# Eight depth pairs by seven products in the late heads, and the weights' parts in two buffers and a third one by phase

## The chip, the cores and the metric

The kernel runs on one core of a Trainium2 chip. The metric is the device time of one execution in microseconds (us), the median of several runs. A profile is one such execution. Its engines are PE (TensorE, the matrix products; PEld is its loading of weights), DVE (VectorE), ACT (ScalarE), POOL (GpSimd, hardly used) and SP (SyncE, which issues the DMAs).

## The reference

A trunk of two layers on 512 tokens of width 2048, all in float32. The first layer is an mLSTM with 8 heads, the second a band attention that reads one K and V, computed from the first layer's result (kv_w). Only the first matters here:

```python
def mlstm_mixer(h, w_in, conv_w, conv_b, gate_b, g_head, w_out):
    proj = h @ w_in
    qk = jax.nn.silu(causal_conv(proj[..., :A_V0], conv_w, conv_b))
    v = proj[..., A_V0:A_O0]
    o = proj[..., A_O0:A_Z0]
    z = proj[..., A_Z0:A_G0]
    ...
    ht = mlstm_chunkwise(heads(qk[..., :A_QK], A_DK), heads(qk[..., A_QK:], A_DK), heads(v, A_DV), li, lf)
    ht = rmsnorm(ht, g_head.reshape(A_HEADS, A_DV)).reshape(Bn, S, A_INNER)
    y = jax.nn.sigmoid(o) * ht * jax.nn.silu(z)
    return y @ w_out
```

Each head has q and k of 256 columns, and v, o and z of 512.

## The kernel before

**Weights.** All weights lie in one stream of pieces of up to 128 x 1024 in the order of their use (stream, L60). wpiece (L188) takes the next one: a DMA into wr, a cast on ACT to the high part wh (L182), and a subtraction on DVE for the low part wl (L183). A product of two float32 matrices is three matmuls, high by high, high by low and low by high (mm3). wh and wl each have three buffers in the pool wp (L146), wr has two, and in some phases every third piece takes its wr from a pool of that phase (spare).

**Products by seven.** proj_s (L273) computes two column tiles at once. For a depth pair (two depth steps of 128) it either takes eight products as they are ("eight", 12 matmuls of 512 columns) or seven with sums of the weights and of the inputs, after Strassen and Winograd ("seven", 21 matmuls of 256). The weights' sums are made in wpiece: L207, L208 and L209 on DVE, then a cast and a subtraction for their parts wsh and wsl. The results come together in four accumulators D, C, A and B, and go to SBUF at L322 to L331. HEAD_PAIRS says how many of the eight depth pairs of a head's call go by seven: 7, the other one by eight, in the call's first piece. The other three pieces have two pairs by seven each ("merged").

**Heads.** The loop over h runs through 8 heads. Heads up to 3 (HALF) have q, k in other ways; head 3 makes the input's sums h1s on the way (head_sums, L598) and brings its o and z calls up by RAMP from 4 to 7 pairs. Heads 4 to 7 each make six calls of proj_s: q, k (names zq) and four for o and z (names zo), with V between (proj_b, four accumulators; its weights have one difference a piece, L214). After q and k stands the convolution (L547 to L549, then SiLU at L552).

**End of a head.** den gives dd, the four numerators ps_n go through L752 (square) and L753 (scaling of zo), the squares' sum sqs is split to sp_q, two matmuls make ps_q, and then comes a chain on one tile dd, in the pool t1: L759, L760 (DVE), a square root (ACT, L761), a reciprocal (DVE, L762), four products zo by dd (L764), each followed by a DMA that writes it to ysc.

**After head 7.** The pool t1 is closed with phA, and a_w_out follows: pieces 290 and up, y read back from ysc (yr), split into y, and ps_y. Piece 290 meets y0_0, the next one y0_1, and so on; the first needs nothing of head 7.

**Order.** Each engine runs its own queue in order. Within the program a scheduler sets that order, by priorities (high_priority, AHEAD = 300). A pool's memory may be that of an earlier pool: a tile then waits for the last use of the tiles that lay there (reuse_waits="tile").

Of the kernel before, what the change touches and what calls it, by code (L numbers as in the profile page):

```python
# [9 lines left out]
F32 = mybir.dt.float32  # L10
F32R = mybir.dt.float32r
# [4 lines left out]
P = 128  # L16
# [24 lines left out]


KEY_PAIRS = [6, 7, 8, 8, 8, 8, 8, 8]
HEAD_PAIRS = 7
RAMP = [4, 5, 6, 7]
HALF = 3
ATT_PAIRS = 8
# [85 lines left out]
def hybrid_trunk(ctx, tc, xT, xN, c, adaT, cols, wst, wg, ext, kc, out):  # L133
    nc = tc.nc
    order = stream()

    const = ctx.enter_context(tc.tile_pool(name="const", bufs=1))
# [5 lines left out]
    def pool(name, bufs=1, **kw):  # L143
        return tc.tile_pool(name=name, bufs=bufs, reuse_waits="tile", **kw)

    wp = ctx.enter_context(tc.tile_pool(name="wp", bufs=3, side="right"))  # L146

    ysc = dram.tile([NH, P, 4, S], F32, name="ysc")
    gsc = dram.tile([2, NH, S], F32, name="gsc")
# [8 lines left out]

    cl = const.tile([P, NCOL], F32, name="cl")
    kcs = const.tile([P, 144], F32, name="kcs")  # L160
    ones_f = const.tile([P, P], F32, name="ones_f")
    cst = const.tile([P, 4], F32, name="cst")
    mod = const.tile([P, 128], F32, name="mod")
    amul = const.tile([P, 3 * KT], F32, name="amul")
# [1 line left out]
    ssq = const.tile([P, 16], F32, name="ssq")  # L166
    rsn = const.tile([P, 4], F32, name="rsn")
    ssum = const.tile([P, S], F32, name="ssum")
    nc.vector.memset(ones_f, 1.0)
    nc.vector.memset(cst[:, 0:1], EPS)  # L170
    nc.vector.memset(cst[:, 1:2], 1.0)
    eps_c, one_c = cst[:, 0:1], cst[:, 1:2]
# [10 lines left out]
        nc.vector.tensor_tensor(lo, src, hi.bitcast(F32), op=ALU.subtract)  # L183

    ahead = [0]
    spare = [None]

    def wpiece(mat, groups=(), pl=None, bufs=(2, 2), diff=False):  # L188

        i, at = wpos
        m, blocks = order[i]
        assert m == mat
        n = sum(w for _, _, w in blocks)
        wpos[:] = i + 1, at + P * n
        with tc.high_priority(ahead[0]):
            own = spare[0] and i % (RAW_BUFS + 1) == 0
            raw = (spare[0] if own else wp).tile([P, 1024], F32, tag="raw", name=f"wr{i}", bufs=1 if own else RAW_BUFS)[:, :n]
            nc.sync.dma_start(raw, wst[at : at + P * n].rearrange("(p n) -> p n", p=P))  # L200
            ts = []
            c0 = 0
            for j, ns in enumerate(groups):
                w = ns * P
                r = raw[:, c0 : c0 + 4 * w]
                t = pl.tile([P, 3 * w], F32, tag="ws", name=f"ws{i}_{j}", bufs=bufs[0])
                nc.vector.tensor_tensor(t[:, : 2 * w], r[:, w : 3 * w], r[:, : 2 * w], op=ALU.subtract)  # L207
                nc.vector.tensor_tensor(r[:, w : 2 * w], t[:, w : 2 * w], r[:, :w], op=ALU.add)  # L208
                nc.vector.tensor_tensor(t[:, 2 * w :], r[:, 3 * w :], r[:, w : 2 * w], op=ALU.subtract)  # L209
                ts.append(t)  # L210
                c0 += 4 * w
            if diff:
                t = pl.tile([P, n // 2], F32, tag="ws", name=f"ws{i}", bufs=1)
                nc.vector.tensor_tensor(t, raw[:, n // 2 :], raw[:, : n // 2], op=ALU.subtract)  # L214
                ts.append(t)
            hi = wp.tile([P, 1024], F32R, tag="hi", name=f"wh{i}")[:, :n]
            lo = wp.tile([P, 1024], F32R, tag="lo", name=f"wl{i}")[:, :n]
            split(hi, lo, raw)
            out = [(hi, lo)]
            for j, t in enumerate(ts):  # L220
                sh = pl.tile(list(t.shape), F32R, tag="wsh", name=f"wsh{i}_{j}", bufs=bufs[1])
                sl = pl.tile(list(t.shape), F32R, tag="wsl", name=f"wsl{i}_{j}", bufs=bufs[1])
                split(sh, sl, t)
                out.append((sh, sl))
        return out
# [47 lines left out]
    def proj_s(mat, xs, ss, f, z1, z2, name, pl, bufs, at={}, merged=False, other=False):  # L273

        D, C, A, B = [(newa if other and n != "d" else newp)(f"ps_{n}{name}") for n in "dcab"]
        pieces = pair_pieces(f, merged)
        begun = set()
        h0, h1_ = slice(0, 256), slice(256, 512)  # L280
        for i, (sk, nk) in enumerate(pieces):
            if i in at:
                at[i]()
            main, *extra = wpiece(mat, [len(ks) for ks in sk], pl, bufs)

            def acc(ps, cols, parts, b, x, last):
                start = id(ps) not in begun
                begun.add(id(ps))
                w = slice(b * P, (b + 1) * P)
                mm3(ps[:, cols], parts[0][:, w], parts[1][:, w], x[:, 0, :], x[:, 1, :], start, last)  # L290

            def eight():
                b0 = 4 * sum(len(ks) for ks in sk)
                for m, k in enumerate(nk):
                    for j in range(2):
                        for t, ps in enumerate((A, B)):
                            acc(ps, slice(0, S), main, b0 + 4 * m + 2 * j + t, xs[2 * k + j], False)

            def seven(g, ks):
                ns = len(ks)  # L300
                b0 = 4 * sum(len(u) for u in sk[:g])
                end = i == len(pieces) - 1 and g == len(sk) - 1
                for ps, cols, t, at_, x, last in (
                    (D, h1_, 0, 1, lambda k: ss[k][1], False),
                    (D, h0, 0, 0, lambda k: xs[2 * k][:, :, h0], end),
                    (C, h0, 1, 1, lambda k: ss[k][2], False),
                    (C, h1_, 1, 0, lambda k: ss[k][0], end),
                    (A, h0, 0, 3, lambda k: xs[2 * k + 1][:, :, h0], False),
                    (A, h1_, 1, 2, lambda k: xs[2 * k + 1][:, :, h1_], end),
                    (B, h0, 0, 2, lambda k: ss[k][3], end),  # L310
                ):
                    if i == 0 and g == 0 and ps is B:
                        eight()
                    for j, k in enumerate(ks):
                        acc(ps, cols, extra[g] if t else main, (0 if t else b0) + at_ * ns + j, x(k), last and j == ns - 1)

            if i:
                eight()
            for g, ks in enumerate(sk):
                seven(g, ks)  # L320
        with tc.high_priority(AHEAD):
            nc.scalar.copy(z1[:, 0, :], D[:, h0])  # L322
            nc.vector.tensor_tensor(z2[:, 1, :], z1[:, 0, :], D[:, h1_], op=ALU.add)
            nc.vector.tensor_tensor(z1[:, 1, :], z2[:, 1, :], C[:, h0], op=ALU.add)
            nc.vector.tensor_tensor(z2[:, 0, :], z2[:, 1, :], C[:, h1_], op=ALU.add)
            nc.vector.tensor_tensor(z2[:, 1, :], z1[:, 1, :], C[:, h1_], op=ALU.add)
            nc.vector.tensor_tensor(z1, z1, A.rearrange("p (a t) -> p a t", a=2), op=ALU.add)
            if f < KT // 2:
                nc.vector.tensor_tensor(z2, z2, B.rearrange("p (a t) -> p a t", a=2), op=ALU.add)
            else:  # L330
                nc.vector.tensor_tensor(z2[:, 0, :], z2[:, 0, :], B[:, h0], op=ALU.add)  # L331
# [42 lines left out]
    phA = ExitStack()  # L374
    tp = phA.enter_context(pool("t1", bufs=3, side="right"))
    mst = ExitStack()
    q1p = mst.enter_context(pool("q1", side="right"))
    ap_ = mst.enter_context(pool("ada", side="right"))

    scB = ap_.tile([P, D], F32, name="scB")  # L380
# [1 line left out]
    acp = hst.enter_context(pool("acc"))  # L382
    st = ExitStack()
    sp = spare[0] = st.enter_context(pool("start"))
    ADA_BUFS = 3

    def ada_load(i, j, p, n, pin=lambda ins: ins):
# [30 lines left out]
    for q in range(4):  # L418
        t = sp.tile([P, 4, S], F32, name=f"xt{q}")
# [45 lines left out]
    h1 = []  # L465
# [130 lines left out]
    h1s = []  # L596
# [10 lines left out]

    def pair(c, name, other, f=HEAD_PAIRS, at={}):
        z1, z2 = (acp.tile([P, 2, 256], F32, tag="so", name=f"{name}_{i}", bufs=6) for i in range(2))
        proj_s("a_w_in", h1, h1s, f, z1, z2, name, hq, (1, 2), at, True, other)  # L610
        return [z.rearrange("p a t -> p (a t)") for z in (z1, z2)]

    def scores(h, j, qk, pr, nm, nmd, tot):
# [30 lines left out]
    for h in range(NH):  # L644
# [20 lines left out]
        if h == HALF:  # L665
            while loaded or pending:
                background(3)
            spare[0] = None
            mst.close()
            hqst = ExitStack()  # L670
            hq = hqst.enter_context(pool("hq", side="right"))
# [13 lines left out]
        at = {8 + 2 * j: lambda j=j: scores(h, j, qk, pr, nm, nmd, tot) for j in range(4)} if h else {}  # L685
# [11 lines left out]
        for m in range(4):  # L697
            with tc.high_priority(AHEAD):
                if m < 3:
                    t = hp.tile([P, 2, S], F32R, tag="qk", name=f"v{h}_{m}", bufs=4)  # L700
                    split(t[:, 0, :], t[:, 1, :], pv[m])
                else:
                    t = hp.tile([P, S], F32, tag="nm", name=f"v{h}_{m}")
# [6 lines left out]
        for i in range(4):  # L710
            if h >= HALF:
                f = HEAD_PAIRS if h > HALF else RAMP[i]
# [58 lines left out]
    hqst.close()  # L771
    hst.close()
    phA.close()


    kst = ExitStack()
# [142 lines left out]
    for pair, ms in enumerate(PAIRS):  # L919
        for g in range(1, 4):  # L920
            at = scale_steps(4, 12, 20, *([28] if g < 3 else [])) if pair == 0 else {}
            if pair == 0 and g == 3:
                at[28] = lambda: (scale_sums(), amul_cols(2, 48 + KT, GPRE + KT))
            if pair == 1 and g == 1:
                at = {2: lambda: residual(0), 4: lambda: residual(1)}
                at |= {20 + 4 * i: lambda i=i: turned(0, [i], False) for i in range(3)}
            if pair == 1 and g == 2:
                at = {2: lambda: turned(0, [3], False)}
# [62 lines left out]
    for i in range(KT // 2):  # L991
        z = zp.tile([P, 4, 256], F32, tag="z", name=f"zk{i}")
        ready = len(hs)
        at = {2: input_sums} if ready < KT // 2 else {}
# [8 lines left out]
    for g in range(2, 4):  # L1003
        n = -(-ATT_PAIRS // 2)
# [280 lines left out]
```

## Time and profile before

| | us |
|---|---|
| median of 3 runs | 2791.75 (2791.1 to 2793.53) |
| profiled execution | 2792.15 |
| its span | 2789.7 |
| PE busy | 2760.0 |
| DVE busy | 2200.9 |
| ACT busy | 1392.4 |

The span is the time from the first to the last instruction in the trace; 2.45 us of the execution lie around it. A row of a timeline has the start, the duration, engine, line and operation, out<-in, how many instructions are put together, and in brackets the idle time before it with what ended it. A matmul's duration overlaps the next one's, so PE's pace is read from start to start. Rows of groups have the busy time in all, the mean of one in ns, and the idle time ahead of them. Times are from the span's start.

### The profile page before, as it was taken

How to read it: one execution, taken by the hardware profiler on the slowest of the kernel's cores; microseconds unless marked ns; L12 is line 12 of the kernel's file. 1: busy time of each engine (PE TensorE's matmuls, PEld its weight loads, DVE VectorE, ACT ScalarE, POOL GpSimd, SP SyncE). 2: the span in 40 equal slices, each digit the busy share in tenths (PEclk: the TensorE clock that was granted, in tenths of full speed). 3: DMA queues.
4: the chain of work that ended last, by engine and by line, in shares of the span. 5: the costliest groups of instructions: out<-in, count | busy, mean ns of one | idle time of the engine just before them, and what ended most of it. 6: DMA issues, size and time to landing. Idle time of an engine off the chain costs nothing.

```text
span 2789.7 us, 42543 instructions
## 1 busy us (share of the span) xinstructions
PE 2760.0 (99%) x16184; PEld 2448.2 (88%) x16184; DVE 2200.9 (79%) x3647; ACT 1392.4 (50%) x2016; POOL 0.2 (0%) x4
## 2 busy tenths in 40 slices
PE   7999999999999999999999999999999999999998
PEld 5887888888998989989999888888999899999887
DVE  6986978769897887878967667567986698989676
ACT  4235524234555554555646344568534466666523
POOL 0000000000000000000000000000000000000000
PEclk9999999999999999999999999999999999999999
DMA  8975697865232332332325788878534533334687
GB/s 290 309 261 181 213 314 254 301 231 174 99 107 100 104 115 91 106 106 99 113 91 196 231 294 298 259 254 292 185 137 174 174 128 125 123 130 128 219 308 243
DMA packets 185015, 527.10 MB, mean 189 GB/s; under 512 B 19893, under 2 KB 38357, under 8 KB 184169
## 3 DMA queue, kind: packets, MB, share of 16 engines
q1 hardware_dynamic: 184810, 524.38, 55.6%
q8 instruction: 126, 2.06, 0.3%
q14 instruction: 79, 0.65, 0.1%
HBM read 490.69 MB, written 38.85 MB: 190 GB/s over the span
## 4 chain that ended last, share of the span: by engine, by line
PE 91%; DVE 4%; DMA 2%; ACT 1%; issue 1%; SPq 0%; DVEq 0%; ACTq 0%
PE ps_y L228 19%; PE ps_v L228 12%; PE ps_azo L228 5%; PE ps_o L228 4%; PE ps_kv L228 4%; PE ps_czo L228 3%; PE ps_dzo L228 3%; PE ps_az L228 3%; PE ps_cz L228 3%; PE ps_dz L228 3%; PE ps_qk L228 3%; PE ps_z L228 3%; PE ps_l L228 3%; PE ps_bzo L228 3%; PE ps_s L228 2%; PE ps_lead L228 2%
## 5 line engine op out<-in xcount | busy, mean ns | idle before, releaser
L182 ACT CAST wh<-wr 128x1024 fp32r<-128x1024 f32 (+3 forms) x586 | 586.9, 1003 | 794.7 <-PE ps_y L228 221.6
L183 DVE TENSOR_TENSOR wl<-wr,wh 128x1024 fp32r<-128x1024 f32 (+3 forms) x586 | 678.9, 1160 | 327.6 <-ACT wh L182 324.9
L228 PE MATMUL ps_y<-wh,y 128*128 128x512 f32 x1536 | 476.0, 390 | 0.0
L228 PEld LDWEIGHTS ps_y<-wh,y 128*128 128x128 f32 x1536 | 288.0, 188 | 59.5
L182 ACT CAST wsh<-ws 128x768 fp32r<-128x768 f32 (+2 forms) x236 | 179.4, 760 | 257.3 <-PE ps_az L228 123.8
L228 PE MATMUL ps_y<-wl,y 128*128 128x512 f32 x768 | 299.0, 389 | 0.0
L228 PE MATMUL ps_v<-wh,h 128*128 128x512 f32 x912 | 289.7, 390 | 0.0
L183 DVE TENSOR_TENSOR wsl<-ws,wsh 128x768 fp32r<-128x768 f32 (+2 forms) x236 | 202.6, 859 | 71.9 <-ACT wsh L182 70.4
L228 PEld LDWEIGHTS ps_v<-wh,h 128*128 128x128 f32 x912 | 171.3, 188 | 35.0
L228 PE MATMUL ps_v<-wl,h 128*128 128x512 f32 x456 | 177.8, 390 | 0.0
L228 PEld LDWEIGHTS ps_y<-wl,y 128*128 128x128 f32 x768 | 144.2, 188 | 29.6
L228 PE MATMUL ps_kv<-wh,hkv 128*128 128x512 f32 x512 | 159.3, 390 | 0.0
L207 DVE TENSOR_TENSOR ws<-wr 128x256 f32<-128x256 f32 (+1 forms) x208 | 132.8, 639 | 9.0 <-DMA wr<-in_wst 7.1
L393 DVE CUSTOM_DVE_ANT_0 ada<-ada,scB,mod 128x1024 f32<-128x1024 f32 x96 | 122.9, 1281 | 18.7 <-DMA ada<-in_adaT 17.7
L393 DVE CUSTOM_DVE_ANT_0 ada<-ada,scB,cl 128x1024 f32<-128x1024 f32 x96 | 122.8, 1280 | 15.9 <-DMA ada<-in_adaT 15.7
L228 PEld LDWEIGHTS ps_kv<-wh,hkv 128*128 128x128 f32 x512 | 96.1, 188 | 19.8
L228 PEld LDWEIGHTS ps_v<-wl,h 128*128 128x128 f32 x456 | 85.7, 188 | 17.6 <-issue 0.9
L228 PE MATMUL ps_kv<-wl,hkv 128*128 128x512 f32 x256 | 100.0, 391 | 0.8 <-DVE wl L183 0.8
L228 PE MATMUL ps_l<-h,wh 128*128 128x512 f32 x320 | 99.0, 391 | 1.3 <-ACT oz L486 1.3
L209 DVE TENSOR_TENSOR ws<-wr 128x128 f32<-128x128 f32 (+1 forms) x208 | 82.7, 398 | 4.0
L208 DVE TENSOR_TENSOR wr<-ws,wr 128x128 f32<-128x128 f32 (+1 forms) x208 | 82.2, 396 | 3.0
L228 PE MATMUL ps_azo<-h,wh 128*128 128x256 f32 (+1 forms) x372 | 84.1, 314 | 0.0
(405 smaller groups left out, 6440.7 us busy)
## 6 DMA issues: line engine op xcount, KB each, us to landing
wr<-in_wst SPq DMA_DIRECT2D x520, 512.0 KB, 3.8
ada<-in_adaT SPq DMA_DIRECT2D x224, 512.0 KB, 6.0
adq<-in_adaT SPq DMA_DIRECT2D x64, 256.0 KB, 5.3
xt<-nsc SPq DMA_DIRECT2D x48, 256.0 KB, 3.3
wr<-in_wst SPq DMA_DIRECT2D x30, 256.0 KB, 4.1
yr<-ysc SPq DMA_DIRECT2D x28, 256.0 KB, 6.4
wr<-in_wst SPq DMA_DIRECT2D x16, 384.0 KB, 6.6
bsc<-in_ext SPq DMA_DIRECT2D x16, 320.0 KB, 6.2
```

The lines of the kernel that those rows point to most:

```text
L182: nc.scalar.copy(hi, src)
L183: nc.vector.tensor_tensor(lo, src, hi.bitcast(F32), op=ALU.subtract)
L207: nc.vector.tensor_tensor(t[:, : 2 * w], r[:, w : 3 * w], r[:, : 2 * w], op=ALU.subtract)
L208: nc.vector.tensor_tensor(r[:, w : 2 * w], t[:, w : 2 * w], r[:, :w], op=ALU.add)
L209: nc.vector.tensor_tensor(t[:, 2 * w :], r[:, 3 * w :], r[:, w : 2 * w], op=ALU.subtract)
L228: nc.tensor.matmul(ps, a, b, start=start, stop=stop)
L393: pin(nc.vector.tensor_tensor_reduce(at, at, (sc or scB)[:, j * D // 2 : (j + 1) * D // 2], 1.0, mod[:, i : i + 1] if j else col(CB + i), ...
```

## The change

1. HEAD_PAIRS is 8: in heads 4 to 7 no pair goes by eight, and the first piece of a call is like the other three. V takes its difference on all eight pieces, and head 3 makes one more h1s.
2. wp has two buffers of hi and lo in place of three. Pieces whose number divides by 3 take theirs from a pool of the phase (spare_w): q1 up to head 3, nothing from there to head 7, and a new pool wx from the end of head 7 to the end of the kernel.
3. The weights' sums ws have two buffers in the heads in place of one.
4. ones_f moves from the constants to the pool of the start.
5. In proj_s the two halves of A change places.

```diff
-HEAD_PAIRS = 7
+HEAD_PAIRS = 8
...
-    wp = ctx.enter_context(tc.tile_pool(name="wp", bufs=3, side="right"))
+    wp = ctx.enter_context(tc.tile_pool(name="wp", bufs=2, side="right"))
...
-    ones_f = const.tile([P, P], F32, name="ones_f")
...
-                t = pl.tile([P, n // 2], F32, tag="ws", name=f"ws{i}", bufs=1)
+                t = pl.tile([P, n // 2], F32, tag="ws", name=f"ws{i}", bufs=bufs[0])
...
-            hi = wp.tile([P, 1024], F32R, tag="hi", name=f"wh{i}")[:, :n]
-            lo = wp.tile([P, 1024], F32R, tag="lo", name=f"wl{i}")[:, :n]
+            pw = spare_w[0] if spare_w[0] and i % 3 == 0 else wp
+            hi, lo = (
+                pw.tile([P, 1024], F32R, tag=t, name=f"{u}{i}", bufs=2 if pw is wp else 1)[:, :n]
+                for t, u in (("hi", "wh"), ("lo", "wl"))
+            )
...
-                    (A, h0, 0, 3, lambda k: xs[2 * k + 1][:, :, h0], False),
-                    (A, h1_, 1, 2, lambda k: xs[2 * k + 1][:, :, h1_], end),
+                    (A, h1_, 1, 2, lambda k: xs[2 * k + 1][:, :, h1_], False),
+                    (A, h0, 0, 3, lambda k: xs[2 * k + 1][:, :, h0], end),
...
-    q1p = mst.enter_context(pool("q1", side="right"))
+    q1p = spare_w[0] = mst.enter_context(pool("q1", side="right"))
...
-        proj_s("a_w_in", h1, h1s, f, z1, z2, name, hq, (1, 2), at, True, other)
+        proj_s("a_w_in", h1, h1s, f, z1, z2, name, hq, (2, 2), at, True, other)
...
-            spare[0] = None
+            spare[0] = spare_w[0] = None
...
     phA.close()
+    spare_w[0] = ctx.enter_context(pool("wx", side="right"))
```

Lines of the new kernel from L182 to L207 stand two lower (a cast of the weights is L180, a lower part L181), those of the heads' end three higher (L759 is L762, the products with dd L767).

Three places where the rows move. First VectorE's queue after head 7, from the split of the squares' sum sp_q7 on; y2, y3 and so on are parts of y, wl of the weights. Before:

```order
L183 TENSOR_TENSOR wl293_14141<-wr293_14138,wh293_14140 128x1024
L183 TENSOR_TENSOR sp_q7_13976<-sqs7_13916,sp_q7_13976 128x512
L183 TENSOR_TENSOR y2_1_0_14236<-yr2_1_0_14232,y2_1_0_14236 128x512
L183 TENSOR_TENSOR y2_1_1_14239<-yr2_1_1_14233,y2_1_1_14239 128x512
L183 TENSOR_TENSOR y3_0_0_14280<-yr3_0_0_14276,y3_0_0_14280 128x512
L183 TENSOR_TENSOR y3_0_1_14283<-yr3_0_1_14277,y3_0_1_14283 128x512
L183 TENSOR_TENSOR wl294_14181<-wr294_14178,wh294_14180 128x1024
L183 TENSOR_TENSOR y3_1_0_14320<-yr3_1_0_14316,y3_1_0_14320 128x512
L183 TENSOR_TENSOR y3_1_1_14323<-yr3_1_1_14317,y3_1_1_14323 128x512
L741 TENSOR_TENSOR dd7_13912<-dd7_13912,ssum_108 128x512
L759 SCALAR_TENSOR_TENSOR dd7_13912<-ps_q7_13975,dd7_13912 128x512
```

And now, from sp_q7 to the first product behind the y parts:

```order
L181 TENSOR_TENSOR sp_q7_14232<-sqs7_14172,sp_q7_14232 128x512
L181 TENSOR_TENSOR y2_0_0_14447<-yr2_0_0_14443,y2_0_0_14447 128x512
L181 TENSOR_TENSOR y2_0_1_14450<-yr2_0_1_14444,y2_0_1_14450 128x512
L181 TENSOR_TENSOR y2_1_0_14495<-yr2_1_0_14491,y2_1_0_14495 128x512
L181 TENSOR_TENSOR y2_1_1_14498<-yr2_1_1_14492,y2_1_1_14498 128x512
L181 TENSOR_TENSOR wl293_14400<-wr293_14397,wh293_14399 128x1024
L181 TENSOR_TENSOR y3_0_0_14539<-yr3_0_0_14535,y3_0_0_14539 128x512
L181 TENSOR_TENSOR y3_0_1_14542<-yr3_0_1_14536,y3_0_1_14542 128x512
L181 TENSOR_TENSOR y3_1_0_14579<-yr3_1_0_14575,y3_1_0_14579 128x512
L181 TENSOR_TENSOR y3_1_1_14582<-yr3_1_1_14576,y3_1_1_14582 128x512
L719 TENSOR_TENSOR zo7_3_0_13922<-zo7_3_0_13922,zo7_3_1_13923 128x512
```

Two parts of y2 and the product for zo7_3 have come behind sp_q7, and wl294 is gone from there.

Second the same queue at the low part wl291 of the second piece of a_w_out. Before, it stood behind the first scaling of zo7, ahead of the rows above:

```order
L329 TENSOR_TENSOR zo7_3_1_13676<-zo7_3_1_13676,ps_bzo7_3_13680 128x512
L716 TENSOR_TENSOR zo7_3_0_13675<-zo7_3_0_13675,zo7_3_1_13676 128x512
L753 SCALAR_TENSOR_TENSOR zo7_0_0_12982<-ps_n7_0_13917,cl_99,zo7_0_0_12982 128x512
L183 TENSOR_TENSOR wl291_14053<-wr291_14050,wh291_14052 128x1024
L183 TENSOR_TENSOR wl292_14097<-wr292_14094,wh292_14096 128x1024
```

Now it stands at the end of head 7's chain:

```order
L762 SCALAR_TENSOR_TENSOR dd7_14168<-ps_q7_14231,dd7_14168 128x512
L756 SCALAR_TENSOR_TENSOR zo7_3_0_13922<-ps_n7_3_14216,cl_99,zo7_3_0_13922 128x512
L763 TENSOR_SCALAR dd7_14168<-dd7_14168 128x512
L765 RECIPROCAL dd7_14168<-dd7_14168 128x512
L767 TENSOR_TENSOR zo7_0_0_13202<-zo7_0_0_13202,dd7_14168 128x512
L767 TENSOR_TENSOR zo7_1_0_13442<-zo7_1_0_13442,dd7_14168 128x512
L767 TENSOR_TENSOR zo7_2_0_13682<-zo7_2_0_13682,dd7_14168 128x512
L767 TENSOR_TENSOR zo7_3_0_13922<-zo7_3_0_13922,dd7_14168 128x512
L181 TENSOR_TENSOR wl291_14312<-wr291_14309,wh291_14311 128x1024
L181 TENSOR_TENSOR y4_0_0_14627<-yr4_0_0_14623,y4_0_0_14627 128x512
```

wl291 has moved behind everything that reads dd7. 291 divides by 3, so its tile is in wx, and it lies on the address of dd7. ScalarE's cast wh291 has likewise moved, behind the square root on dd7.

Third PE's queue around ps_q7. Before, both matmuls of ps_q7 stood within piece 292:

```order
L228 MATMUL ps_y0_0_2_14010<-wl292_14097,y1_0_0_14104 128x512
L228 MATMUL ps_q7_13975<-sp_q7_13976,ones_r_1802 128x512 [waits Activation_49]
L228 MATMUL ps_y0_0_2_14010<-wh292_14096,y1_0_0_14104 128x512
L228 MATMUL ps_y0_0_3_14011<-wh292_14096,y1_0_0_14104 128x512
L228 MATMUL ps_q7_13975<-sp_q7_13976,ones_r_1802 128x512 [waits DVE_49]
L228 MATMUL ps_y0_0_3_14011<-wl292_14097,y1_0_0_14104 128x512
```

Now they stand between piece 290 and piece 291:

```order
L229 MATMUL ps_y0_0_3_14270<-wl290_14274,y0_0_1_14282 128x512
L229 MATMUL ps_y0_0_3_14270<-wh290_14273,y0_0_1_14282 128x512
L229 MATMUL ps_q7_14231<-sp_q7_14232,ones_r_1802 128x512 [waits Activation_49]
L229 MATMUL ps_q7_14231<-sp_q7_14232,ones_r_1802 128x512 [waits DVE_49]
L229 MATMUL ps_y0_0_0_14267<-wh291_14311,y0_1_0_14317 128x512 [waits Activation_49]
L229 MATMUL ps_y0_0_1_14268<-wh291_14311,y0_1_0_14317 128x512
L229 MATMUL ps_y0_0_0_14267<-wl291_14312,y0_1_0_14317 128x512 [waits DVE_49]
```

Pieces 291 and 292 no longer stand ahead of ps_q7, and PE's third matmul of piece 291 waits for wl291.

More of the change, by code (lines that the diff above doesn't have):

```diff
@@ L168, in hybrid_trunk @@
     ssum = const.tile([P, S], F32, name="ssum")
-    nc.vector.memset(ones_f, 1.0)
     nc.vector.memset(cst[:, 0:1], EPS)
@@ L185, in hybrid_trunk @@
     ahead = [0]
-    spare = [None]
+    spare, spare_w = [None], [None]
     def wpiece(mat, groups=(), pl=None, bufs=(2, 2), diff=False):
@@ L384, in hybrid_trunk @@
     sp = spare[0] = st.enter_context(pool("start"))
+    ones_f = sp.tile([P, P], F32, name="ones_f")
+    nc.vector.memset(ones_f, 1.0)
     ADA_BUFS = 3
```

## The prediction

> **What bounds the kernel now.** The page comes first: busy shares, granted clock, and the chain that ended last.
>
> ```profile
> PE 2760.0 (99%) x16184; PEld 2448.2 (88%) x16184; DVE 2200.9 (79%) x3647; ACT 1392.4 (50%) x2016; POOL 0.2 (0%) x4
> ...
> PEclk9999999999999999999999999999999999999999
> ...
> PE 91%; DVE 4%; DMA 2%; ACT 1%; issue 1%; SPq 0%; DVEq 0%; ACTq 0%
> ```
>
> PE is busy in 99% of the span and carries 91% of the last chain, so the time is PE's matmuls plus the little that it waits. The list of PE's waits says how little:
>
> ```profile
> PE ps_lead L228 <- ACT wh L182: 4.1, 1, 4.1
> ...
> PE ps_n L228 <- DVE zo L753: 1.4, 2, 0.8
> ...
> PE ps_dzq L228 <- DVE wl L183: 1.1, 3, 0.4
> ```
>
> The largest one lies in the lead, before the heads. At the start of the late heads (ps_dzq) it waits 1.1 us in all, and around head 7's end (ps_n, once 0.8) as little. So whatever the change takes from PE's own work comes off the time nearly in full, and whatever new wait it gives PE is added nearly in full. The other engines matter only where PE comes to wait for them. By the busy time of three stretches (head 5's start, its gates, the end of head 7) cover is thin in one:
>
> ```profile
> core 0: us, PE busy (x) PEld busy (x) DVE busy (x) ACT busy (x) POOL busy (x), PEclk, DMA share, GB/s
> 993.00:1015.00 22.00, 21.55 (x164) 20.52 (x163) 21.19 (x34) 13.30 (x18) 0.00 (x0) 1.00 0.27 95
> 1066.00:1147.00 81.00, 81.00 (x633) 78.99 (x632) 62.98 (x101) 40.46 (x48) 0.00 (x0) 1.00 0.29 99
> 1505.00:1545.00 40.00, 39.19 (x187) 32.74 (x187) 31.48 (x42) 23.14 (x32) 0.00 (x0) 1.00 0.87 291
> ```
>
> In the gates VectorE has 18 us free of 81; at the head's start it is busy for 21.19 of 22.
>
> **Part 1: eight products against seven.** In a gate projection of head 4, one piece with the pair of eight and one with two pairs of seven read so on PE:
>
> ```profile
> 1067.34 0.63 PE L228 MATMUL ps_azo<-h,wh 128*128 128x512 f32 x2
> ...
> 1070.09 0.40 PE L228 MATMUL ps_bzo<-h1s,wh 128*128 128x256 f32 x2
> ...
> 1070.44 0.40 PE L228 MATMUL ps_dzo<-h1s,wh 128*128 128x256 f32 x2
> ...
> 1075.48 0.40 PE L228 MATMUL ps_dzo<-h1s,wh 128*128 128x256 f32 x2
> ```
>
> The pair by eight products runs from 1067.34 to 1070.09: 2.75 us for 12 matmuls of 512. Two pairs by seven take 1070.44 to 1075.48, 5.04 us for 42 of 256, so 2.52 a pair. Each call of proj_s gains 0.23 us. Heads 4 to 7 make six such calls each (q, k, four gates), 24 in all: **−5.5 us**. This is PE work, so it is kept wherever PE doesn't wait.
>
> VectorE pays for it. The first piece of a call is now cut like the others, by these forms of the groups (from head 4's V to head 5's gates):
>
> ```profile
> L183 DVE TENSOR_TENSOR wl<-wr,wh 128x1024 fp32r<-128x1024 f32 x29 | 35.5, 1223 | 22.5 <-ACT wh L182 22.5
> L183 DVE TENSOR_TENSOR wsl<-ws,wsh 128x768 fp32r<-128x768 f32 x15 | 14.2, 948 | 3.2 <-ACT wsh L182 3.2
> L207 DVE TENSOR_TENSOR ws<-wr 128x512 f32<-128x512 f32 x16 | 11.0, 688 | 0.3
> ...
> L183 DVE TENSOR_TENSOR wsl<-ws,wsh 128x384 fp32r<-128x384 f32 x6 | 3.3, 556 | 0.6 <-ACT wsh L182 0.6
> ...
> L329 DVE TENSOR_TENSOR zo<-zo,ps_bzo 128x512 f32<-128x512 f32 x4 | 2.7, 680 | 0.0
> ...
> L207 DVE TENSOR_TENSOR ws<-wr 128x256 f32<-128x256 f32 x6 | 2.5, 422 | 0.1
> ...
> L208 DVE TENSOR_TENSOR wr<-ws,wr 128x128 f32<-128x128 f32 x6 | 1.7, 290 | 0.1
> ```
>
> L207 grows by 0.27 us (688 against 422), the lower split by 0.39 (948 against 556), and two additions from 128 to 256 wide by 0.13 each (422 against 290, the 256-wide price taken from L207's row); the last addition, of B, halves and saves about 0.26. Net some 0.65 us a call. In the gates the 18 free us hide it. The cast of one hi part is, on ScalarE:
>
> ```profile
> 1520.47 1.04 ACT L182 CAST wh<-wr 128x1024 fp32r<-128x1024 f32 x1
> ```
>
> With two buffers of hi and lo parts in place of three, a part frees when PE leaves the piece two back; then come the cast (1.04) and the 1.22 of wl, 2.26 us, while PE works 5.04 on the piece between. That leaves some 2.8 us for queues, so I take no stall there, nor in V, whose pieces are 24 matmuls of 512, 5.5 us at the pace above. The eighth difference of V adds a subtraction of 512 and a split, on the same cover.
>
> At a late head's start nothing is free: q and k add 1.3 us to VectorE, PE's work shrinks by 0.46. Against that, two ws buffers let the weights' casts go ahead of the convolution in both queues, and A's swapped halves free the extra parts a product sooner. Bounds: the 1.1 us of waits go (with their slack, −2 us over four heads), or all of 1.3 + 0.46 lands on PE each time (+7). I take half a microsecond a head, **+2 us**, nearer to no change since the waits shown were small. Head 3, with two buffers and one more head_sums, has no such tight place in the trace; it is inside these bounds.
>
> **Part 2: the way from head 7 into a_w_out.** Here the change moves wl291, the lower part of the second piece of a_w_out. Its new tile comes from the pool wx, on memory that t1 gave back, where dd7 lives to the end of head 7's normalisation. VectorE's queue now has wl291 behind the four products with dd7; before, it stood ahead of the whole chain. PE's queue holds piece 290, both sums ps_q7, two matmuls of wh291 and then wl291: nothing else may pass. What the chain costs, the rows of before tell (VectorE first, then ScalarE):
>
> ```profile
> 1523.71 0.69 DVE L183 TENSOR_TENSOR sp_q<-sqs,sp_q 128x512 fp32r<-128x512 f32 x1 [0.27 <-ACT sp_q L182]
> 1524.32 2.49 DVE L183 TENSOR_TENSOR y<-yr,y 128x512 fp32r<-128x512 f32 x4
> 1526.76 1.23 DVE L183 TENSOR_TENSOR wl<-wr,wh 128x1024 fp32r<-128x1024 f32 x1
> ...
> 1530.49 0.69 DVE L759 SCALAR_TENSOR_TENSOR dd<-ps_q,dd 128x512 f32<-128x512 f32 x1 [0.70 <-ACT dd L742]
> 1531.21 0.43 DVE L760 TENSOR_SCALAR dd<-dd 128x512 f32<-128x512 f32 x1
> ...
> 1534.64 3.35 DVE L762 RECIPROCAL dd<-dd 128x512 f32<-128x512 f32 x1 [0.72 <-ACT dd L761]
> ...
> 1539.77 1.89 DVE L764 TENSOR_TENSOR zo<-zo,dd 128x512 f32<-128x512 f32 x3
> ```
> ```profile
> 1533.97 0.64 ACT L761 ACTIVATE dd<-dd 128x512 f32<-128x512 f32 x1
> ```
>
> And PE's side:
>
> ```profile
> 1506.13 3.78 PE L228 MATMUL ps_n<-p,v 128*128 128x512 f32 x22
> ...
> 1512.55 2.06 PE L228 MATMUL ps_n<-p,v 128*128 128x512 f32 x11 [0.81 <-DVE zo L753]
> ...
> 1517.86 2.08 PE L228 MATMUL ps_n<-p,v 128*128 128x512 f32 x11
> ...
> 1523.20 0.62 PE L228 MATMUL ps_y<-wh,y 128*128 128x512 f32 x2
> ...
> 1523.88 0.62 PE L228 MATMUL ps_y<-wh,y 128*128 128x512 f32 x2
> ```
>
> In the time of before: PE starts ps_n at 1506.13. The 44 matmuls go at about 0.165 us each (22 in some 3.6), the fourth group without its gap now, and end about 1513.4. Piece 290 is 24 matmuls at 0.227 (three from 1523.20 to 1523.88), 5.45 us: 1518.8. The sums ps_q7 need sp_q. Before, the last group of ps_n started at 1517.86 between two pieces and ended about 1519.7, and sp_q's lower part ran 4 us later, at 1523.71. Now that group ends at 1513.4, so sp_q comes at 1517.4 at the earliest; with the y parts that stand ahead of it on ScalarE and VectorE I take 1519.1. The sums end near 1519.8, and PE has two matmuls of wh291 left.
>
> VectorE first goes through what now stands between: four y parts (2.49), wl293 (1.2), four more (2.49), to 1525.3. Then zo7_3's product, L759, zo7_3's scaling and L760, some 2.4 us: 1527.7. ScalarE's root 0.64, its table load already done meanwhile: 1528.3. Reciprocal 3.35: 1531.7. Four products at 0.63 (1.89 for three): 1534.2. wl291, 1.2: **1535.4**. PE stands from 1519.8 to 1535.4, 15.6 us; the two matmuls in it are worth 0.45 and the gap of 0.81 goes: net **+14.3 us**. None of this can be made up, since PE is full both sides of it.
>
> Bounds: with no y parts in VectorE's way, the chain alone is 0.69 + 0.43 + 0.64 + 3.35 + 2.5 + 1.2, about 9 us (+8). If ScalarE or the y loads are late too, 18. I keep 14.3, because the rows in between are printed in its queue.
>
> **What the clock does after it.** The lead shows PE's speed behind a long wait:
>
> ```profile
> 29.72 1.22 PE L228 MATMUL ps_lead<-h,wh 128*128 128x512 f32 x2 [4.14 <-ACT wh L182]
> 30.74 0.77 PE L228 MATMUL ps_lead<-h,wl 128*128 128x512 f32 x1
> 31.30 1.05 PE L228 MATMUL ps_lead<-h,wh 128*128 128x512 f32 x2
> ...
> 35.14 0.64 PE L228 MATMUL ps_lead<-h,wh 128*128 128x512 f32 x2
> 35.62 0.40 PE L228 MATMUL ps_lead<-h,wl 128*128 128x512 f32 x1
> ```
>
> From 31.30 to 35.14 nine matmuls of 512 take 0.427 us each; the next two together 0.48 (35.14 to 35.62). From 29.72 on twelve are slow, and against 0.227 cost 0.2 each: **+2.4 us**, which I add once behind the 15 us stall (bounds 0 and 2.7). The granted-clock row shows 9 in this slice all the same, so it won't show it after the change either. The gap of 0.81 at 1512.55 brought no such slowness. The Trainium skill ("TensorE: Matmul & The Clock Gate", Part 1) says that PE's clock falls to half after an idle window of about 3.4 us and comes back after as long a busy one; that would make an estimate of 1.7 us of it, and a sum 0.7 lower, where the rows of the lead say 2.4.
>
> **The sum**, against the profiled execution's own 2792.15 (span 2789.7 and 2.45 around it): −5.5 + 14.3 + 2.4 + 2 = +13.2. On the median of 2791.75: **2805.0 us**.
>
> **Rivals.** *A, not slower: the stall is short.* If VectorE gets to head 7's chain at once, and PE waits only the 9 us of the bare chain, without slow matmuls behind it, and the late heads' starts gain their 2 us: −5.5 + 8 − 2 = +0.5, 2792. For it: before had the y parts run while the chain waited for ps_q, so they may be early again. Against it: they are queued between sp_q and L759 in order, and their casts on ScalarE too. It decides the sign when the stall falls under about 7.5 us. Chance 0.10, nearly all of it within 0.2% of no change. *B, the two buffers bite:* if each of the 24 calls waits 0.4 us (a queue over the 2.8 us of slack), +9.6 comes on top in place of the +2: 2812.6. For it: VectorE's 21.19 of 22 at the heads' starts; against it: the 18 us free in the gates, where 16 of the calls are. Chance 0.12. *C, the gain without the loss:* PE's −5.5 alone, 2786.3, if wx's first tile didn't lie on dd7's memory; the queue shows that it does. Chance 0.04.
>
> **Numbers.** A measurement of this kernel can tell about 0.2%, 5.6 us, from no change. My case has 0.74: 2805, its own range 2798 to 2810: stalls of 10 to 18 are 8.7 to 16.7 net, with 0.5 to 4.5 for the heads' starts. With B's half, 8 in 10 lie within 2796 to 2812. Slower by over 0.2% (above 2797.3): my case nearly whole and B, 0.85; within 0.2%: A and the lowest of mine, 0.11; faster: 0.04.
>
> **What would show it.** Right: one wait of PE in ps_y for wl of 14 to 16 us just after ps_q7, with wl291 right behind the fourth product with dd7; matmuls of 0.43 us for some 5 us behind it; a pair of pieces in the gates without 512-wide matmuls; the late heads each some 1.4 us shorter where nothing waits. Wrong: no PE wait above 5 us after head 7, or PE waits for wl and wsl in every late call that add up to over 5 us.

## The result, and the profile after

The changed kernel takes 2808.73 us (median of 4 runs, 2806.36 to 2810.34) against 2792.64 before: a ratio of 1.0056, 95% interval 1.0044 to 1.0068. It is 16.1 us slower; 13.2 slower was forecast. The profiled execution took 2808.36 us, with a span of 2806.6.

First the page: PE's busy time, the granted clock by slice, and the chain that ended last.

```profile
PE 2761.2 (98%) x16400; PEld 2455.8 (88%) x16400; DVE 2220.3 (79%) x3664; ACT 1408.2 (50%) x2023; POOL 0.2 (0%) x4
...
PEclk9999999999999999999998999999999999999999
...
PE 88%; DVE 5%; DMA 4%; ACT 2%; issue 1%; SPq 0%; DVEq 0%; ACTq 0%
```

PE's share of the last chain fell from 91 to 88%, and one slice, from 1473 to 1544, shows a lower clock. The list of PE's waits names the place:

```profile
PE ps_y L229 <- ACT wh L180: 9.2, 1, 9.2
PE ps_y L229 <- DVE wl L181: 5.1, 1, 5.1
...
PE ps_n L229 <- DVE zo L756: 1.8, 2, 1.6
...
PE ps_t L1092 <- DVE s L1083: 1.0, 2, 0.6
```

Two waits that were not there before, one behind the other, 14.3 us together. VectorE's timeline from the split of sp_q7 on shows the forecast chain in its forecast order:

```profile
1509.66 0.69 DVE L181 TENSOR_TENSOR sp_q<-sqs,sp_q 128x512 fp32r<-128x512 f32 x1 [0.17 <-ACT sp_q L180]
1510.27 2.49 DVE L181 TENSOR_TENSOR y<-yr,y 128x512 fp32r<-128x512 f32 x4
...
1519.19 3.35 DVE L765 RECIPROCAL dd<-dd 128x512 f32<-128x512 f32 x1 [0.69 <-ACT dd L764]
1522.58 2.50 DVE L767 TENSOR_TENSOR zo<-zo,dd 128x512 f32<-128x512 f32 x4
1525.18 1.23 DVE L181 TENSOR_TENSOR wl<-wr,wh 128x1024 fp32r<-128x1024 f32 x1
```

The lower part of piece 291 comes right behind the four products with dd7. On PE's side the first row is both sums, and the others are piece 291 (the two matmuls of wh291 stand at 1520, between the waits):

```profile
1509.99 0.91 PE L229 MATMUL ps_q<-sp_q,ones_r 128*128 128x512 f32 x2
...
1526.46 0.79 PE L229 MATMUL ps_y<-wl,y 128*128 128x512 f32 x1 [5.09 <-DVE wl L181]
1527.48 0.63 PE L229 MATMUL ps_y<-wl,y 128*128 128x512 f32 x1
...
1528.76 0.63 PE L229 MATMUL ps_y<-wl,y 128*128 128x512 f32 x1
...
1532.07 0.39 PE L229 MATMUL ps_y<-wl,y 128*128 128x512 f32 x1
...
1532.75 0.39 PE L229 MATMUL ps_y<-wl,y 128*128 128x512 f32 x1
```

From 1510.9 to 1526.46 are 15.6 us, as worked out ahead. Three matmuls then take 1.28 us (1527.48 to 1528.76), 0.427 each, and later 0.68, 0.227 each. The twelve from 1526.46 to 1531.61 take 5.15 us, 2.4 more than at 0.227. Stretches of that time, with the granted clock behind PE's busy time:

```profile
core 0: us, PE busy (x), PEclk, DMA share, GB/s
...
1511.00:1513.00 2.00, 0.00 (x0) 1.00 0.99 361
1513.00:1514.00 1.00, 0.00 (x0) 1.00 1.01 389
1514.00:1515.00 1.00, 0.00 (x0) 0.68 0.69 186
1515.00:1526.00 11.00, 1.22 (x2) 0.50 0.93 309
...
1530.00:1531.00 1.00, 1.00 (x4) 0.50 1.05 299
1531.00:1532.00 1.00, 1.00 (x5) 0.79 0.96 371
1532.00:1535.00 3.00, 3.00 (x15) 1.00 0.50 154
```

By the two mixed rows the clock falls to half at 1514.36 and comes back at 1531.42: 3.5 us after PE stops (1510.9), and 5 us after it starts again.

To see where else time went, I set marks on PE's timeline: the first matmul of ps_d at the ends of heads 3 and 7, the first of ps_kv, the first and last of ps_dz in the attention heads, and the last of all. In the kernel before they start at 788.03, 1505.66, 1866.88, 2208.69, 2594.32 and 2781.02. The table has, for each kernel, how much longer (+) each stretch between two marks is than in the kernel before.

| profiled kernel | to the end of head 3 | heads 4 to 7 | head 7 to kv | kv to attention | attention heads | the rest | sum |
|---|---|---|---|---|---|---|---|
| changed | −2.4 | −6.4 | +16.7 | +1.1 | +5.8 | +2.0 | +16.9 |
| r1_skip291 | −2.1 | −6.7 | +3.1 | +0.2 | +5.2 | +0.9 | +0.5 |
| r2_a_back | −0.9 | −3.4 | +16.4 | −0.3 | +0.1 | +0.4 | +12.3 |
| r3_both | +0.3 | −3.9 | +3.3 | +0.6 | +0.1 | +0.4 | +0.8 |
| r4_before_swap | +0.7 | −5.7 | −0.7 | −0.2 | +4.4 | +1.8 | +0.3 |
| r5_mix | +0.6 | −6.9 | −1.2 | +0.4 | +0.1 | +0.8 | −6.3 |
| r6_b_headswap | −1.2 | −5.2 | −0.6 | −1.6 | +0.1 | +1.3 | −7.2 |
| r7_mix7 | −0.5 | −4.8 | −1.2 | −0.8 | +0.1 | +0.8 | −6.3 |
| r8_g8 | −2.4 | −1.8 | −1.0 | −1.2 | +0.1 | +6.9 | +0.6 |
| r9_warm | +1.9 | −7.8 | +13.5 | −0.1 | +6.1 | +0.4 | +14.0 |
| r10_ws1 | −0.2 | +1.5 | −1.2 | −0.7 | +0.1 | +3.5 | +3.0 |

Three things stand out in the first row: the heads gained, head 7's end lost, and the attention heads, of which the prediction said nothing, lost 5.8. How much a profile varies by itself, r9 says: up to head 7 it is the changed kernel's program, and the first column differs by 4.3 us (loads at the start), the second by 1.4. So the first column is not read at all, the second and those of +2 or less not closer than some 1.5 us. A profile is one execution: those of r6, r8 and r10 lie 3.2 us under, 4.7 over and 3.4 over the medians of their kernels.

### The profile page after: what moved, and what is told of

It reads as the page before. It is cut to its first block, busy times and chain, and to the rows that moved or that the text cites. A ratio compares the mean times of both kernels' runs of the same rounds, so it can differ in the third digit from the quotient of the medians.

```text
span 2806.6 us, 42903 instructions
## 1 busy us (share of the span) xinstructions
PE 2761.2 (98%) x16400; PEld 2455.8 (88%) x16400; DVE 2220.3 (79%) x3664; ACT 1408.2 (50%) x2023; POOL 0.2 (0%) x4
## 4 chain that ended last, share of the span: by engine, by line
PE 88%; DVE 5%; DMA 4%; ACT 2%; issue 1%; SPq 0%; DVEq 0%; ACTq 0%
PE ps_y L229 16%; PE ps_v L229 12%; PE ps_azo L229 4%; PE ps_o L229 4%; PE ps_kv L229 4%; PE ps_czo L229 4%; PE ps_dzo L229 4%; PE ps_qk L229 3%; PE ps_z L229 3%; PE ps_l L229 3%; PE ps_az L229 3%; PE ps_cz L229 3%; PE ps_dz L229 3%; PE ps_bzo L229 2%; PE ps_s L229 2%; PE ps_lead L229 2%
## 5 line engine op out<-in xcount | busy, mean ns | idle before, releaser
L180 ACT CAST wh<-wr 128x1024 fp32r<-128x1024 f32 (+3 forms) x586 | 585.7, 1001 | 751.2 <-PE ps_y L229 220.4
L181 DVE TENSOR_TENSOR wl<-wr,wh 128x1024 fp32r<-128x1024 f32 (+3 forms) x586 | 678.4, 1159 | 257.7 <-ACT wh L180 255.6
L180 ACT CAST wsh<-ws 128x768 fp32r<-128x768 f32 (+2 forms) x240 | 188.8, 787 | 309.5 <-DVE ws L207 102.0
L181 DVE TENSOR_TENSOR wsl<-ws,wsh 128x768 fp32r<-128x768 f32 (+2 forms) x240 | 215.1, 898 | 87.0 <-ACT wsh L180 85.2
L205 DVE TENSOR_TENSOR ws<-wr 128x512 f32<-128x512 f32 (+1 forms) x208 | 139.4, 671 | 31.4 <-DMA wr<-in_wst 29.9
L207 DVE TENSOR_TENSOR ws<-wr 128x256 f32<-128x256 f32 (+1 forms) x208 | 85.7, 413 | 2.7
L206 DVE TENSOR_TENSOR wr<-ws,wr 128x256 f32<-128x256 f32 (+1 forms) x208 | 85.5, 411 | 1.8
L229 PE MATMUL ps_qk<-h,wh 128*128 128x512 f32 x256 | 79.4, 390 | 0.0
```

What stands on the lines that cost most here:

```text
L180: nc.scalar.copy(hi, src)
L229: nc.tensor.matmul(ps, a, b, start=start, stop=stop)
```

## The experiments

**r1: the second piece elsewhere.** The theory: the wait is for dd7's memory. The rival: head 7's chain is waited for in any case.

```diff
-            pw = spare_w[0] if spare_w[0] and i % 3 == 0 else wp
+            pw = spare_w[0] if spare_w[0] and i % 3 == 0 and i != 291 else wp
```

> The changed kernel, but piece 291 takes its hi and lo parts from the common pool as its neighbours do; the first piece in the new pool is then 294. Theory (the stall after head 7 is the wait of wh291 and wl291 for the memory of dd7, 14.3 us idle and 2.4 us of slow matmuls): about 16.7 us under the changed kernel, so 2792, and no wait of PE over 2 us in ps_y. Rival (PE must wait for head 7's chain in any case, the wait only moves to a later piece): 2800 or more, with a wait of 5 us or more in ps_y.

2791.86 us, ratio to before 1.000 (0.9991 to 1.0010): 16.9 under the changed kernel. The stretch from head 7 to kv fell from +16.7 to +3.1. The rest is a wait at piece 294, whose tile is now the first in the new pool. ScalarE's casts first, then PE:

```profile
1527.02 1.99 ACT L180 CAST wh<-wr 128x1024 fp32r<-128x1024 f32 x2 [4.39 <-PE ps_y L229]
```
```profile
1526.55 0.39 PE L229 MATMUL ps_y<-wh,y 128*128 128x512 f32 x1
1529.07 1.37 PE L229 MATMUL ps_y<-wh,y 128*128 128x512 f32 x4 [2.12 <-ACT wh L180]
...
1531.10 0.63 PE L229 MATMUL ps_y<-wh,y 128*128 128x512 f32 x1
1531.53 0.63 PE L229 MATMUL ps_y<-wl,y 128*128 128x512 f32 x1
1531.96 0.63 PE L229 MATMUL ps_y<-wh,y 128*128 128x512 f32 x1
```

2.1 us of waiting, and behind it matmuls 0.43 us apart again. PE starts piece 294 when the second of the two casts ends (1529.01). The first had stood in ScalarE's queue until PE was done with piece 293, so it is a later piece's, and wh294 stands behind it. So the stall of 14.3 us was that memory, and PE need not wait for head 7's chain. What is left comes from the place of wh294 in the queue; that the memory under the new pool gives it that place is likely, since it is gone with the pool from piece 300 on (r5), but not shown by itself.

**r2: A's halves in their old order,** r1's line as changed.

```diff
-                    (A, h1_, 1, 2, lambda k: xs[2 * k + 1][:, :, h1_], False),
-                    (A, h0, 0, 3, lambda k: xs[2 * k + 1][:, :, h0], end),
+                    (A, h0, 0, 3, lambda k: xs[2 * k + 1][:, :, h0], False),
+                    (A, h1_, 1, 2, lambda k: xs[2 * k + 1][:, :, h1_], end),
```

> The changed kernel with the two halves of A back in their old order, all else as changed. Theory (in the attention heads the new order of A lets the transposes ps_t come in the middle of A's group, and there PE loses the 5.8 us by which the changed kernel falls back between the first and the last product of b_w_in): 5.8 us under the changed kernel, 2803, and the offset against the kernel before stays level through the attention heads. Rival (the third buffer in the new pool costs it): no change, 2808.7, offset still grows by 5 to 6 us there.

2804.25 us, ratio 1.0040 (1.0025 to 1.0055), 4.5 under the changed kernel. The attention heads' loss is gone (+0.1), and the heads gain 3 us less, all of it in head 5 (see r3). By whole times the intervals of the two kernels overlap; the stretches tell them apart. What the order does in the attention heads is seen in the waits ahead of the transposes ps_t. Before:

```profile
L1088 PE MATMUL ps_t<-kcs,s x160: 270/272/328, 2250.8 to 2614.9; 128*128 128x128 f32 x160
...
  DVE pt L183: 1.4, 3
```

Changed:

```profile
L1092 PE MATMUL ps_t<-kcs,s x150: 270/272/331, 2259.8 to 2617.5; 128*128 128x128 f32 x150
...
  DVE pt L181: 4.2, 14
  DVE s L1083: 3.0, 6
```

These lines count the waits of PE and of its weight loads (PEld) together: of the 7.2 us 1.8 are PE's own, and of the 1.4 before 0.4. What PE lost its starts tell: from mark to mark, the steps into, between and out of the transposes take 23.8 us in place of 18.0, and all other steps 367.7 in both kernels. That is the 5.8 of the table. With A's halves swapped, the transposes stand in PE's queue in the middle of A's matmuls, and in the old order behind them, a few matmuls later, when s and pt are there.

**r3: both edits.**

> Both edits at once: piece 291 from the common pool, A's halves in the old order. If the two losses are separate they add up: 16.7 + 5.8 us under the changed kernel, 2786, which is some 6 us faster than the kernel before. If one hides in the other, or the third buffer is what costs in the attention heads: 2790 or more.

2791.66 us, ratio 0.9991 (0.9981 to 1.0001), not the 2786 of the sum. The two losses did add up (−13.4 and −5.7 by the table). What I left out: r1's 3.1 stayed, and without the swap head 5 takes 2.2 us longer than before (r2: 2.5), with it 0.5 and 0.7 less (changed kernel, r1). In both profiles without the swap PE waits 3 us at head 5's start, behind VectorE, and the clock is at half for 3.4 us after it:

```profile
1010.70 0.69 DVE L212 TENSOR_TENSOR ws<-wr 128x512 f32<-128x512 f32 x1 [2.99 <-DMA wr<-in_wst]
```
```profile
1013.57 0.38 PE L229 MATMUL ps_dzq<-h1s,wl 128*128 128x256 f32 x1 [3.02 <-DVE wl L181]
```

The first row is the difference of V's first piece. The second ws buffer lets it stand far ahead in VectorE's queue, and there it waits for its load, with the lower part that PE needs behind it. In the changed kernel, r1, r5 and r9, which have the swap, VectorE does not wait there. How the swap brings that load earlier no run shows.

**r4: the kernel before with A's halves swapped,** the diff of r2 the other way round.

> The kernel before with nothing but A's halves swapped. Theory: about 5.8 us lost in the attention heads, up to 1 us won at the late heads' starts, so 2797 to 2798.5 against 2792.6. Rival (third buffer): no change or up to 2 us faster, 2790.5 to 2792.6. The lead is the same program as before, so its offset in the trace shows what the lead varies by itself from run to run.

2791.95 us, ratio 0.9999 (0.9990 to 1.0008). The expectation of 2797 was wrong in one term. The attention heads lost 4.4, but heads 4 to 7 won 5.7, where up to 1 was expected. The same 4875 matmuls, from ps_d of head 3 to that of head 7, before:

```profile
788.03:1505.66 717.63, 715.72 (x4875) 667.26 (x4874) 582.59 (x916) 386.98 (x503) 0.00 (x0) 1.00 0.30 104
```

and in r4:

```profile
788.73:1500.63 711.90, 711.90 (x4875) 665.87 (x4874) 581.45 (x912) 385.74 (x502) 0.00 (x0) 1.00 0.31 105
```

In r4 PE is busy for all of it. Before, the page listed waits of under 2 us in that stretch; the rest of the 5.7 was within its busy time, as matmuls that started later than the one ahead of them allowed.

**r5: the repaired version.** The new pool from piece 300 on, and the swap in the calls of the first layer alone.

```diff
-            pw = spare_w[0] if spare_w[0] and i % 3 == 0 else wp
+            pw = spare_w[0] if spare_w[0] and i % 3 == 0 and not 290 < i < 300 else wp
...
-                    (A, h1_, 1, 2, lambda k: xs[2 * k + 1][:, :, h1_], False),
-                    (A, h0, 0, 3, lambda k: xs[2 * k + 1][:, :, h0], end),
+                    *(
+                        (A, u, 1 if u is h1_ else 0, 2 if u is h1_ else 3, lambda k, u=u: xs[2 * k + 1][:, :, u], n == 1 and end)
+                        for n, u in enumerate((h1_, h0) if mat == "a_w_in" else (h0, h1_))
+                    ),
```

> The changed kernel, with the new pool used only from piece 300 on, and A's halves swapped in the calls of the first layer's heads alone. Theory (stall of 16.7 us by the memory of dd7, still 4 us of it when piece 294 lay there; 5 us by the swap in the attention heads; 6.4 us gained in heads 4 to 7): no wait of PE over 1 us in ps_y, level through the attention heads, 2785 to 2786, 6 us faster than the kernel before. Rival (two buffers make their own waits in a_w_out, or the slack that the swap took in the attention heads is lost there anyway): 2789 or more.

2784.49 us, ratio 0.9971 (0.9959 to 0.9982): faster than both kernels, 24.2 us under the changed one. PE does not wait in ps_y, and the attention heads are level.

**r6: the kernel before with that swap alone** (r5's second piece of diff).

> The kernel before (seven pairs, three buffers) with A's halves swapped in the heads of the first layer alone. Theory (the swap by itself ends the waits at the starts of heads 4 to 7, 5.7 us, and costs only in the attention heads): 2786, as fast as the one above, all of it at the starts. Rival (the gain of the changed kernel's heads needs the eight pairs): 2790 or more.

2787.37 us, ratio 0.9976 (0.9967 to 0.9985). Seven pairs and three buffers with a swap of two lines get most of it. In the table r6 is the shorter of the two, but its profile was among its fastest. The intervals of r5 and r6 overlap, so the order of the two stays open.

**r7: r5 with HEAD_PAIRS 7.**

> The first one here with HEAD_PAIRS 7 again: two buffers, the swap in the heads, the new pool from piece 300 on, but one pair of each call by eight. Theory (eight pairs by seven take 5.5 us off PE, of which VectorE's fuller starts give back 4 to 5): within 1.5 us of the first one, with the gates 0.9 us a head longer and the starts 0.7 to 1 us shorter. Rival (PE's 5.5 us are kept in full): 5 us slower than the first one.

2786.73 us, ratio 0.9981 (0.9971 to 0.9990). In the table the heads are 2.1 us longer than in r5. By PE's starts each head's four gates are 0.88 us longer, 3.5 in all, which is the 0.23 a call of the prediction; the starts are 1.4 shorter. So eight pairs keep about 2 of their 5.5 us by the profiles; by whole times the intervals overlap.

**r8: r5 with eight pairs in the gates only.**

```diff
-                tile_s("a_w_in", c, c + P, HEAD_PAIRS, True)
+                tile_s("a_w_in", c, c + P, 7, True)
...
-                    zs = pair((i // 2) * (V0 // 2) + h * DK, f"zq{h}_{i}", i > 0)
+                    zs = pair((i // 2) * (V0 // 2) + h * DK, f"zq{h}_{i}", i > 0, 7)
```

> The first one here with eight pairs by seven in the gates only; q and k go by seven pairs and one by eight, as before. Theory (the gates have VectorE's cover and keep 0.9 us a head, the starts have none): gates as short as in the first one, starts as short as in the second, so 2 to 3.5 us faster than both, 2782.5 to 2784. Rival (two buffers, not the number of pairs, crowd the starts): no faster than the first one.

2787.38 us, ratio 0.9981 (0.9971 to 0.9990): no faster than r5. The profiled execution, 2792.05, was its slowest and doesn't stand for the median; but it shows what can happen at a start. VectorE waits for a load that comes late, and PE for VectorE:

```profile
1139.27 0.69 DVE L205 TENSOR_TENSOR ws<-wr 128x512 f32<-128x512 f32 x1 [2.61 <-DMA wr<-in_wst]
```
```profile
1147.99 5.42 PE L229 MATMUL ps_n<-p,v 128*128 128x512 f32 x22 [2.54 <-DVE zo L758]
```

22 matmuls of ps_n take 5.42 us here, with the clock down, and 3.78 elsewhere. The 6.9 us of the last column are a late load too: at 2664 PE waits 3.8 us for VectorE, and VectorE 4.1 for its load. Whether q and k are better with seven pairs stays open.

**r9: PE kept busy through the stall.** The 62 matmuls go into an accumulator that nothing reads.

```diff
+        return t
...
-        sums(ps, sqs, f"q{h}", *((AHEAD, 80) if h == NH - 1 else ()))
+        t = sums(ps, sqs, f"q{h}", *((AHEAD, 80) if h == NH - 1 else ()))
+        if h == NH - 1:
+            keep = newa("ps_keep")
+            with tc.high_priority(-80):
+                for n in range(62):
+                    mm(keep, ones_r, t[:, n % 2, :], n == 0, n == 61)
```

> The changed kernel with 62 more matmuls of 512 columns on PE right behind ps_q7, on sp_q7 and ones, into an accumulator that nothing reads: 14.1 us of work in the place of the wait. Theory (PE's slow matmuls behind the wait come from its idleness, and the wait itself is set by wl291): wl291 comes no later than in the changed kernel, piece 291 runs at 0.227 us a matmul from its first one, and the time is 2.4 us lower than the changed kernel's, 2806. Rival (the slowness comes from the restart itself, by what PE loads or by the 12 parts that come in a burst): piece 291 again has some 12 matmuls of 0.43 us, and the time stays at 2808.7 or rises.

2805.43 us, ratio 1.0047 (1.0030 to 1.0064). On PE:

```profile
1513.64 14.00 PE L229 MATMUL ps_keep<-sp_q,ones_r 128*128 128x512 f32 x61
1527.47 1.07 PE L229 MATMUL ps_y<-wh,y 128*128 128x512 f32 x4
1528.87 0.50 PE L229 MATMUL ps_y<-wl,y 128*128 128x512 f32 x1 [0.32 <-DVE wl L181]
1529.20 0.39 PE L229 MATMUL ps_y<-wh,y 128*128 128x512 f32 x1
1529.43 0.40 PE L229 MATMUL ps_y<-wl,y 128*128 128x512 f32 x1
```

Piece 291 runs at 0.23 us a matmul from the start, and head 7 to kv takes 3.2 us less than in the changed kernel (+13.5 against +16.7): more work on PE, and a shorter stretch. (By whole times the intervals of the two overlap.) The slowness came from the idleness. Not all of the 3.2 is the pace: wl291 comes 0.5 us sooner after ps_d here, and four matmuls of wh291 run ahead of it instead of two.

**r10: r5 with one buffer of ws.**

```diff
-                t = pl.tile([P, n // 2], F32, tag="ws", name=f"ws{i}", bufs=bufs[0])
+                t = pl.tile([P, n // 2], F32, tag="ws", name=f"ws{i}", bufs=1)
...
-        proj_s("a_w_in", h1, h1s, f, z1, z2, name, hq, (2, 2), at, True, other)
+        proj_s("a_w_in", h1, h1s, f, z1, z2, name, hq, (1, 2), at, True, other)
```

> The repaired version (new pool from piece 300 on, A swapped in the heads alone) with one buffer of ws instead of two for the head pairs and V's difference. Theory (the second ws buffer is what lets the late heads' starts hide VectorE's fuller first pieces): starts of heads 4 to 7 0.5 to 1 us longer each, gates the same, 2 to 4 us slower than the repaired version, 2787 to 2788.5. Rival (two ws buffers only move VectorE's work ahead and make it wait for late loads): no slower, 2784.5 or less.

2791.10 us, ratio 0.9998 (0.9988 to 1.0008): 6.6 slower than r5, more than expected. The waits at the starts are there at once:

```profile
PE ps_dzq L229 <- DVE wl L181: 3.0, 5, 0.9
PE ps_dzq L229 <- ACT wh L180: 2.4, 4, 0.6
```

In the table heads 4 to 7 are 8.4 us longer than in r5, all of it at their starts: the second ws buffer is what makes eight pairs bearable at all.

## Why the prediction was right, and where not

**The stall: right in place, cause and size.** Forecast 15.6 us from the end of ps_q7 to wl291, measured 15.6. r1 shows that the memory of dd7 was the cause, since with piece 291 elsewhere 13.6 of the 16.7 are gone.

**The slow matmuls: right, with luck in the size and the lead misread.** Forecast +2.4; the twelve behind the stall cost 2.4, and r9 shows that they are slow for PE's idleness. But the lead was no measure of it. Behind the same wait of 4.1 us the lead has 12 slow matmuls in the profile before, 6 in the changed kernel's and 13 in r6's. Nor does it show that the wait made PE slow: ps_c's matmuls of 512 columns, from 2.16 us on, are 0.85 us apart, and ps_li's, float32 and 512 columns as well, at 228, 0.43: PE seems to have been at half pace from its first ones. The prediction also took it that the granted clock would not show the slowness, since it had not in the lead. The trace before has no entry of the clock ahead of 35.16 us, and a stretch without one reads 1.00:

```profile
29.00:35.14 6.14, 5.42 (x12) 1.00 0.52 161
```

After the change it shows, at 0.50. The Trainium skill ("TensorE: Matmul & The Clock Gate", Part 1) has the fall after an idle window of some 3.4 us. The 3.5 us of the changed kernel agree with that. r1 differs: there a wait of 2.1 us was enough.

**Eight products against seven: right as PE's work.** The gates are 0.88 us a head shorter, the forecast 0.23 a call. (The gate rows that the prediction puts down to head 4 are those of head 5, and VectorE's groups are from head 5's V to head 6's start; the forms are the same.)

**The late heads' starts: mis-sized.** The prediction took +2 for them and bounded the gain at −2, because the page's list of waits had only 1.1 us there. The sum of the heads was −6.4, where −5.5 + 2 was forecast, so the term came out at −0.9. r4 shows that more could be gained there than the list says: the swap alone is worth 5.7 in the kernel before, most of it not in the list of waits. In the changed kernel it is not the swap that gains this. By head, against the kernel before:

| | head 4 | head 5 | head 6 | head 7 |
|---|---|---|---|---|
| changed | −1.4 | −0.5 | −2.2 | −2.3 |
| r2, r3 (no swap) | −1.6, −1.1 | +2.5, +2.2 | −1.9, −2.5 | −2.5, −2.5 |
| r4 (swap alone) | −1.1 | −1.6 | −1.5 | −1.5 |
| r5 | −1.8 | −0.5 | −2.4 | −2.3 |
| r10 (r5, one ws buffer) | −0.2 | +0.8 | 0.0 | +0.9 |

Without the swap heads 4, 6 and 7 gain as much, and only head 5 loses. With one ws buffer (r10) every head is longer than in r5, by 1.2 to 3.1 us. So with eight pairs the second ws buffer keeps the starts short, and the swap keeps head 5's. Against that, r5 and r7 differ by 2.1 where PE's work differs by 5.5, so VectorE's fuller first pieces give back some 3.4, over half of it at head 5's start. A list of waits is a lower bound of what PE lost in a stretch; the same matmuls' starts would have told.

**The attention heads: left out.** The step that failed is the swap's: the prediction costed it for the heads alone ("A's swapped halves free the extra parts a product sooner"), though proj_s serves the attention queries too: the second layer, which the description of the reference leaves aside, matters here. The runs show +5.8 there, gone in r2, r3 and r5, present in r4 without any of the other edits. It is what took the time from the forecast 2805 to 2808.7, together with 3.1 us in the stretches on both sides, less the 2.9 that the heads did better and the 2.4 of the first stretch.

**The rivals.** A (a short stall) did not come true: VectorE did the y parts first, as printed. B (0.4 us for each of 24 calls) neither: the gates lost nothing. C (no stall) did not.

What stays open is head 5's start, where the changed kernel waits 1.6 us in ps_n and heads 6 and 7 do not. A late load, as in r8, would do it: VectorE waits 1.56 us for one at 957.57. But r5 has a wait of 1.64 us in the same ps_n with only 0.53 of VectorE's for a load, so the load alone doesn't explain it. More buffers of raw weights were not tried.

## What to carry to other kernels

A buffer in a pool that opens on freed memory is only free when the last reader of that memory is done: look what lay there, and what stands ahead of its first use in the queues of the engines. A reordering in a shared helper has to be costed at every caller. Where an engine is 99% busy, judge a stretch by the starts of the same instructions in both profiles, since the waits that are listed can be a third of what is lost.

## What the runs showed of the hardware

A wait of 2.1 us (r1) or 2.5 us (r8) on PE was followed by matmuls at half speed, as 15.6 us were, while one of 1.6 us in the changed kernel's ps_n was not. The granted clock tells more. It is at half for 17.07 us in the changed kernel, and for 3.41, a fifth of it, in r1, r3 and r8. Counted from these changes in steps of 3.41 us, the step with the wait of 1.6 us, the step ahead of the fall and the half clock read so in the changed kernel:

```profile
968.23:971.64 3.41, 1.88 (x12) 1.00 0.51 154
1510.95:1514.36 3.41, 0.00 (x0) 1.00 0.96 357
1514.36:1531.43 17.07, 6.19 (x14) 0.50 0.96 313
```

In r1, where the clock fell only after PE was working again (1529.07):

```profile
1526.51:1529.92 3.41, 1.28 (x6) 1.00 1.02 391
1529.92:1533.33 3.41, 3.34 (x9) 0.50 1.02 369
1533.33:1536.00 2.67, 2.67 (x13) 1.00 1.01 387
```

And ahead of r8's fall:

```profile
1145.71:1149.12 3.41, 1.12 (x5) 1.00 0.44 154
```

So in these traces the clock fell behind a step in which PE was busy for 0, 1.12 or 1.28 us of 3.41, and not behind one of 1.88. Of two steps with 1.60 us, one in r3 (from 1532.77) was followed by a fall and one in r10 (from 75.44) was not, so the limit is near half a step; no run places it more closely.

So a short wait can cost nearly twice its length. In r1 2.1 us of waiting made 3.8 us more than r4 has in the same stretch: 3.41 us at half clock lose 1.7, an estimate from the rows above.
